# Four projections over one pass of the k tiles, and the scores of two head pairs as one block, in a hybrid HGRN and attention block on one core

## Chip, cores, metric

The kernel runs on one core of one Trainium2 chip. The metric is the device time of one execution in microseconds (us); smaller is better. TensorE, VectorE, ScalarE, GpSimd (POOL) and SyncE (SP) are called PE, DVE, ACT, POOL and SP in the profile.

## The reference

One block of a streaming encoder, fp32, for 256 tokens of width 2048: a mixer of two branches side by side, merged by gates, and after it a squared-ReLU MLP.

```python
def mixer_block(u, w_in, lb, hg_norm_w, rel_bias, w_branch_a, w_branch_b, w_out):
    z = u @ w_in
    hq, hf, hi, hg, aq, ak, av, gates = jnp.split(z, SPLIT_POINTS, axis=-1)
    g = lb + (1.0 - lb) * jax.nn.sigmoid(hf)
    log_g, kk = jnp.log(g), 1.0 - g
    q = jax.nn.silu(hq) * (HG_DK ** -0.5)
    o = hgrn2_scan(q, kk, hi, log_g)                       # 8 heads of 128
    y_a = rms_norm(o, hg_norm_w) * jax.nn.silu(hg)
    y_b = chunk_band_attention(aq, ak, av, rel_bias)       # 16 heads of 64: softmax(q k / 8 + bias) v
    gate_a, gate_b = jnp.split(jax.nn.sigmoid(gates), 2, axis=-1)
    return (gate_a * (y_a @ w_branch_a) + gate_b * (y_b @ w_branch_b)) @ w_out
...
h = x + mixer_block(rms_norm(x, norm_mix_w), ...)
u = rms_norm(h, norm_mlp_w)
h = h + jnp.square(jax.nn.relu(u @ w_up)) @ w_down
return rms_norm(h, norm_final_w)
```

(Heads and shapes are left out above.) The scan's chunks have 64 tokens; with 256 tokens the attention reaches all earlier chunks, and its bias depends on the clipped distance of query and key.

## The kernel before

**Products.** Every fp32 operand is split in two: a high part, rounded by ACT (`split`, L91; now and then by DVE), and a low part, the difference, by DVE (L92). A product is then high by high plus the two mixed terms. The names in the profile follow this: `raw` is a weight tile as loaded by SP (six buffers), `wh` and `wl` its high and low part (four buffers each), `act_x` both parts of the input. `mm3` (L141 to L143) makes a product whose weights are the moving operand, in three matmuls of 512 columns; `mm_t` (L183, L188) makes a transposed one, with the weights stationary. `weights` is the generator that loads and splits; `tc.high_priority` and `tc.issue_after` tell a scheduler where an instruction is to stand in its engine's order. On each engine instructions run strictly in that order.

**Start.** The HGRN projections hf and hq have 1024 columns each, in halves: hf0, hq0, hf1, hq1. The first three are multiplied side by side: a loop over the k tiles loads and splits two k tiles of x (one at a time at the very start) and then gives each projection its matmuls (`for i in range(3)`). Their sums lie in PSUM: hf0 and hq0 in the four banks of `ps_acc`, hf1 in the two of `ps_sm`. After the loop `add_parts` (L194 to L197) makes f0 and q0, the squares of x give 1/rms (`rstd`), and `rows` (to L314) spreads it over the columns with two transposes on PE. Only then hq1 is multiplied, alone, by `gemm_t` over all 16 k tiles; during this time f and q of the first halves are scaled and go through sigmoid, log and exp (`hf_pair`, `hq_pair`). The projections hi and hg follow, and within them the first HGRN scores (L455, L479, L552), whose last operand is `ql` (L545). ACT loads another table of functions when it goes from sigmoid to log, silu or exp (ACT_TABLE_LOAD).

**Attention.** Four units of the gate and attention projections (av, qk, ga0, ga2; each a product made of block products, whose weight blocks and their sums and differences have names such as p21A, p21B, p21D and r_8) each carry the attention of four heads, as two pairs. The steps are hung into the unit's slots, a slot being 12 matmuls of `mm3`, by tables such as `at_slots((2, p0[0]), (4, p0[1]), (7, ...), (9, ...))`: at slot 2 the first pair, at slot 4 the second, at 7 and 9 their transposes, and the values at the start of the next unit. `attn_pair` (L686 to L727) does for a pair: eight small matmuls for the scores (L694; two heads of 64 rows run side by side on the array's halves) into the one buffer of `ps_sc`; POOL loads the bias (two DMAs, L698, and a memset, L699) into `bias`, a tile with one buffer; DVE adds it (L705, one instruction for columns 0 to 127 and one for the rest), takes the maximum (L707), ACT the exp (L710), DVE the reciprocal (L712) and the multiplication (L714); the transposes on PE (L720, `tpp`) come when their slot calls for them. In between DVE makes the low parts of the unit's weights and adds partial sums (L908).

## Time and profile before

| what | value |
|---|---|
| time, median of 3 runs | 1363.72 us (1363.05 to 1364.31) |
| profiled execution | 1363.58 us, of which the span from the first to the last instruction is 1361.9 us |
| busy PE / DVE / ACT / POOL | 1350.3 / 1166.9 / 970.7 / 156.3 us |
| mean granted clock of TensorE | 0.998 |
| DMA | 336.92 MB, mean 247 GB/s |

The profile shows one execution. A row of a timeline has the start, the length, the engine, the line of the kernel, the operation, its output and inputs, and in brackets the idle time ahead of it on its engine, with what ended it. Where rows of one line follow each other, they are drawn as one with their number (x2), and their lengths overlap a little, since an engine starts on an instruction before the one ahead has ended. TensorE's matmuls overlap likewise: their spacing, not their length, is what one costs.

### The profile page before, as it was taken

What the parts mean: (1) busy time and instruction counts of PE and PEld (TensorE: products, weight loads), DVE (VectorE), ACT (ScalarE), POOL (GpSimd) and SP (SyncE); (2) the same over time, 40 slices, a digit from 0 to 9 for tenths busy, and PEclk for the clock granted to TensorE, in tenths of its full rate; (3) what the DMA queues carried; (4) which work ended last, traced back from release to release, by engine and by line L of the source; (5) the groups of instructions that cost most, each with busy time, mean ns of one, the idle gap of its engine ahead of it and who ended that gap; (6) DMA issues with size and microseconds to landing.
All of it is one profiled execution on the core that took longest, in us unless ns stands there. A gap on an engine that the chain in (4) does not pass through costs nothing.

```text
span 1361.9 us, 19182 instructions
## 1 busy us (share of the span) xinstructions
PE 1350.3 (99%) x6753; PEld 1116.1 (82%) x6753; DVE 1166.9 (86%) x1406; ACT 970.7 (71%) x1299; POOL 156.3 (11%) x239
## 2 busy tenths in 40 slices
PE   9999999999999999999999999999999999999997
PEld 7888888878778888888888888888888888888886
DVE  6888977887888988798998889898889988899885
ACT  6877765776777666556778767787667876678764
POOL 3000000110110000110121011100121001110210
PEclk9999999999999999999999999999999999999999
DMA  9655557778885988869898889998899988999892
GB/s 347 228 185 157 176 181 264 217 211 258 247 225 171 307 276 246 262 153 325 286 278 264 244 254 263 281 306 225 245 281 275 301 222 238 294 292 274 260 279 97
DMA packets 132498, 336.92 MB, mean 247 GB/s; under 512 B 11296, under 2 KB 14624, under 8 KB 132016
## 3 DMA queue, kind: packets, MB, share of 16 engines
q1 hardware_dynamic: 110816, 266.11, 56.4%
q0 software_dynamic: 21296, 69.28, 26.2%
q8 instruction: 53, 0.87, 0.2%
q14 instruction: 45, 0.37, 0.1%
q10 hardware_dynamic: 288, 0.29, 0.1%
HBM read 271.67 MB, written 10.49 MB: 207 GB/s over the span
## 4 chain that ended last, share of the span: by engine, by line
PE 98%; DMA 1%; ACT 0%; DVE 0%; issue 0%; SPq 0%; POOL 0%; POOLq 0%; DVEq 0%
PE acc_hq L183 2%; PE acc_hf L183 2%; PE tp_u L110 1%; PE acc_hq L188 1%; PE acc_hg L143 1%; PE acc_hi L143 1%; PE acc_hg L141 1%; PE acc_hi L142 1%; PE acc_hg L142 1%; PE acc_ga2c L141 1%; PE acc_hi L141 1%; PE acc_hf L188 1%; PE acc_ga0c L141 1%; PE acc_avc L141 1%; PE acc_dn30c L141 1%; PE acc_wo2c L143 1%
## 5 line engine op out<-in xcount | busy, mean ns | idle before, releaser
L183 PE MATMUL acc_hq<-act_x,wh_hq 128*128 128x512 f32 x128 | 41.0, 399 | 1.5 <-ACT wh_hq L91 1.2
L183 PE MATMUL acc_hf<-act_x,wh_hf 128*128 128x512 f32 x128 | 40.6, 398 | 0.4 <-DVE wh_hf L91 0.4
L1339 POOL DMA_DIRECT2D hd<-y x24 | 24.7, 1041 | 45.8 <-ACT y L1338 45.4
L188 PEld LDWEIGHTS acc_hf<-act_x,wl_hf 128*128 128x128 f32 x128 | 23.4, 188 | 5.4
L188 PEld LDWEIGHTS acc_hq<-act_x,wl_hq 128*128 128x128 f32 x128 | 23.4, 188 | 5.3 <-DVE wl_hq L92 0.2
L141 PE MATMUL acc_hg<-wh_hg,act_x 128*128 128x512 f32 x64 | 25.1, 392 | 0.0
L141 PE MATMUL acc_hi<-wh_hi,act_x 128*128 128x512 f32 x64 | 25.0, 391 | 0.0
L143 PE MATMUL acc_hg<-wh_hg,act_x 128*128 128x512 f32 x64 | 24.9, 390 | 0.0
L143 PE MATMUL acc_hi<-wh_hi,act_x 128*128 128x512 f32 x64 | 24.9, 389 | 0.0
L142 PE MATMUL acc_hi<-wl_hi,act_x 128*128 128x512 f32 x64 | 24.9, 389 | 0.0
L142 PE MATMUL acc_hg<-wl_hg,act_x 128*128 128x512 f32 x64 | 24.9, 389 | 0.0
L92 DVE TENSOR_TENSOR wl_hq<-raw_hq,wh_hq 128x1024 fp32r<-128x1024 f32 (+2 forms) x21 | 20.1, 966 | 5.4 <-ACT wh_hq L91 5.4
L188 PE MATMUL acc_hq<-act_x,wl_hq 128*128 128x256 f32 x128 | 24.6, 279 | 0.0
L188 PE MATMUL acc_hf<-act_x,wl_hf 128*128 128x256 f32 x128 | 24.6, 279 | 0.0
L92 DVE TENSOR_TENSOR wl_hf<-raw_hf,wh_hf 128x512 fp32r<-128x512 f32 (+2 forms) x26 | 20.9, 811 | 4.1 <-ACT wh_hf L91 3.9
L91 ACT CAST wh_hq<-raw_hq 128x1024 fp32r<-128x1024 f32 (+2 forms) x21 | 17.6, 842 | 8.9 <-DMA raw_hq<-in_w_in_t_dram 4.6
L92 DVE TENSOR_TENSOR act_u<-tp_u,act_u 128x512 fp32r<-128x512 f32 x28 | 19.2, 685 | 5.3 <-ACT act_u L91 5.3
L100 POOL TENSOR_TENSOR ro<-os,mhalf 128x4 f32<-128x4 f32 x4 | 4.4, 1099 | 167.4 <-DVE os L99 164.3
L92 DVE TENSOR_TENSOR wl_hg<-raw_hg,wh_hg 128x1024 fp32r<-128x1024 f32 x16 | 19.4, 1219 | 3.0 <-ACT wh_hg L91 3.0
L183 PEld LDWEIGHTS acc_hq<-act_x,wh_hq 128*128 128x128 f32 x128 | 19.9, 189 | 2.2 <-ACT wh_hq L91 1.4
L183 PEld LDWEIGHTS acc_hf<-act_x,wh_hf 128*128 128x128 f32 x128 | 19.9, 190 | 1.0 <-DVE wh_hf L91 0.7
L91 ACT CAST wh_hf<-raw_hf 128x512 fp32r<-128x512 f32 (+2 forms) x24 | 17.5, 740 | 4.4 <-PE acc_hg L143 1.6
(2295 smaller groups left out, 5327.3 us busy)
## 6 DMA issues: line engine op xcount, KB each, us to landing
raw_hi<-in_w_in_n_dram SPq DMA_DIRECT2D x16, 512.0 KB, 3.8
raw_hg<-in_w_in_n_dram SPq DMA_DIRECT2D x16, 512.0 KB, 3.7
raw_hq<-in_w_in_t_dram SPq DMA_DIRECT2D x12, 512.0 KB, 5.2
hd<-y POOLq DMA_DIRECT2D x24, 256.0 KB, 8.6
raw_hf<-in_w_in_t_dram SPq DMA_DIRECT2D x16, 256.0 KB, 5.6
raw_hf<-in_w_in_t_dram SPq DMA_DIRECT2D x8, 512.0 KB, 4.0
raw_aq<-in_w_in_t_dram SPq DMA_DIRECT2D x8, 512.0 KB, 4.4
raw_ak<-in_w_in_t_dram SPq DMA_DIRECT2D x8, 512.0 KB, 4.3
```

The costliest lines, as they stand in the source:

```text
L91: casts[:] = [(copy or nc.scalar.copy)(hi, src)]
L92: low[:] = [nc.vector.tensor_tensor(lo, src, hi.bitcast(F32), op=ALU.subtract)]
L100: nc.gpsimd.tensor_tensor(dst, ms, mhalf[:, :width], op=ALU.pow)
L110: nc.tensor.transpose(tp[:, j, :], src[:, j * P:(j + 1) * P], ident)
L141: nc.tensor.matmul(acc, hi, wh, start=first, stop=False, skip_group_check=True)
L142: nc.tensor.matmul(acc, hi, wl, start=False, stop=False, skip_group_check=True)
L143: newest[:] = [nc.tensor.matmul(acc, lo, wh, start=False, stop=last, skip_group_check=True)]
L183: newest[:] = [nc.tensor.matmul(acc[cb], wh[:, cb * P:(cb + 1) * P], r.rearrange("p u t -> p (u t)"), start=kt == 0, stop=last)]
L188: newest[:] = [nc.tensor.matmul(acc[cb][:, 0:T], wl[:, cb * P:(cb + 1) * P], r[:, 0, :], start=False, stop=False)]
L1339: nc.gpsimd.dma_start(hd[n][m], t, accum_op=ALU.add)
```

## The change

Two things. First, hq1 joins the loop at the start as a fourth projection; its sums lie in the two banks of `ps_tp`, so the transposes of rstd move to `ps_sm`, and behind the sums of all four projections. hq1's weights are thereby loaded in smaller pieces, as those of the others. Second, `attn_scores` makes the scores of both pairs of a unit at the slot of the first pair: the first pair's into two banks of `ps_tp`, one for each head, the second pair's into `ps_sc`. `attn_pair` begins at the bias; for the first pair the add is made of four instructions (one for each head and span), for the second of two as before. The steps of the units qk and ga2 move by one slot.

```diff
                 nc.scalar.copy(dst[:, cb, :], acc[cb][:, T:])
-                nc.vector.tensor_tensor(dst[:, cb, :], acc[cb][:, 0:T], dst[:, cb, :], op=ALU.add)
+                added = nc.vector.tensor_tensor(dst[:, cb, :], acc[cb][:, 0:T], dst[:, cb, :], op=ALU.add)
+        return added
 
...
     xT = [new_act(f"x{c}") for c in range(4)]
-    accs = [new_acc("hf0"), new_acc("hq0"), [ps_sm.tile([P, NC], F32, name=f"acc_hf1{j}", tag="sm") for j in range(2)]]
+    accs = [new_acc("hf0"), new_acc("hq0")] + [[pool.tile([P, NC], F32, name=f"acc_{what}{j}", tag=tag) for j in range(2)]
+                                               for what, pool, tag in (("hf1", ps_sm, "sm"), ("hq1", ps_tp, "tp"))]
     ws = [weights(w_in_t, C_HF, KD, T, "hf0", (1, 1) + (2,) * 7, first=True),
           weights(w_in_t, C_HQ, KD, T, "hq0", (1, 1) + (2,) * 7),
-          weights(w_in_t, C_HF + T, KD, T, "hf1", (1, 1) + (2,) * 7)]
+          weights(w_in_t, C_HF + T, KD, T, "hf1", (1, 1) + (2,) * 7),
+          weights(w_in_t, C_HQ + T, KD, T, "hq1", (1, 1) + (2,) * 7)]
     steps = [1, 1] + [2] * (KD // 2 - 1)
...
 
-    done = [0, 0, 0]
+    done = [0] * 4
     for kt, n in zip(starts, steps):
...
                                                       op0=ALU.mult, op1=ALU.subtract)
-        for i in range(3):
+        for i in range(4):
             with ExitStack() as es:
...
         nc.vector.tensor_copy(wide, bc(factors, 2, P))
-        tp = ps_tp.tile([P, NM, P], F32, name=f"tp_{what}", tag="tp")
+        tp = ps_sm.tile([P, NM, P], F32, name=f"tp_{what}", tag="sm")
         for m in range(NM):
...
 
-    f0, z0 = h2("f0"), h2("zq0")
-    add_parts(f0, accs[0])
-    add_parts(z0, accs[1])
+    f0, z0, f1, z1 = [h2(what) for what in ("f0", "zq0", "f1", "zq1")]
+    for i, t in enumerate((f0, z0, f1, z1)):
+        added = add_parts(t, accs[i])
     for m in range(NM):
...
     rsqrt(rstd, xsq, D, NM)
-    rstd_t = rows(rstd, "rstd")
+    with tc.issue_after(added.ins):
+        rstd_t = rows(rstd, "rstd")
     rstd8 = const.tile([P, T], F32, name="rstd8")[:, 0:NM]
     nc.vector.tensor_scalar(rstd8, rstd, 0.125, None, op0=ALU.mult)
-
-    f1, z1 = h2("f1"), h2("zq1")
-    add_parts(f1, accs[2])
-    add_parts(z1, gemm_t(xT, w_in_t, C_HQ + T, KD, "hq1"))
 
...
 
-    def attn_pair(g, pr, qT, kT):
+    SPANS = (slice(0, P), slice(P, 3 * P))
+
+    def attn_scores(g, p0, qT, kT):
+
+        first = [ps_tp.tile([P, NC], F32, name=f"s{g}{p0}{j}", tag="tp") for j in range(2)]
+        second = ps_sc.tile([P, 2, NC], F32, name=f"s{g}{p0 + 1}", tag="sc")
+        both = (first, [second[:, j, :] for j in range(2)])
+        with tc.issue_after(newest[0].ins), tc.high_priority(offset=2000):
+            for d, q, k in zip(SPANS, (slice(0, P), slice(P, T)), (slice(0, P), slice(0, T))):
+                for p in range(2):
+                    for j in range(2):
+                        r = slice(64 * j, 64 * j + 64)
+                        nc.tensor.matmul(both[p][j][:, d], qT[r, p0 + p, q], kT[r, p0 + p, k], start=True, stop=True)
+        return ([lambda d, j=j: (slice(j, j + 1), first[j][:, d].rearrange("p (j t) -> p j t", j=1)) for j in range(2)],
+                [lambda d: (slice(0, 2), second[:, :, d])])
+
+    def attn_pair(g, pr, scores):
 
         n = g * 4 + pr
-        sc = ps_sc.tile([P, 2, NC], F32, name=f"s{g}{pr}", tag="sc")
-        with tc.issue_after(newest[0].ins), tc.high_priority(offset=2000):
-            for d, q, k in ((slice(0, P), slice(0, P), slice(0, P)), (slice(P, 3 * P), slice(P, T), slice(0, T))):
-                for j in range(2):
-                    r = slice(64 * j, 64 * j + 64)
-                    nc.tensor.matmul(sc[:, j, d], qT[r, q], kT[r, k], start=True, stop=True)
         bias = bp.tile([P, 2, T], F32, name=f"bias{n}", tag="bias", bufs=1)
...
         s = bp.tile([P, 2, 3 * P], F32, name=f"sb{n}", tag="s", bufs=2)
-        spans = (slice(0, P), slice(P, 3 * P))
+        spans = SPANS
         mx = small.tile([P, 2, 2], F32, name=f"mx{n}", tag="mx")
...
         for d in spans:
-            nc.vector.tensor_tensor(s[:, :, d], sc[:, :, d], rev(bias[:, :, 0:d.stop - d.start]), op=ALU.add)
+            for part in scores:
+                j, sc = part(d)
+                nc.vector.tensor_tensor(s[:, j, d], sc, rev(bias[:, j, 0:d.stop - d.start]), op=ALU.add)
         for b, d in enumerate(spans):
...
         g, p0 = i // 2, i % 2 * 2
-        turns, pts = [], []
+        turns, pts, got = [], [], []
+
+        def scores():
+            got.extend(attn_scores(g, p0, qkT[f"q{g}"], qkT[f"k{g}"]))
 
         def pair(p):
-            qT, kT = [qkT[f"{name}{g}"][:, p0 + p, :] for name in "qk"]
-            turns.extend(attn_pair(g, p0 + p, qT, kT))
-
-        return ([lambda p=p: pair(p) for p in range(2)], [lambda j=j: pts.append(turns[j]()) for j in range(4)],
+            turns.extend(attn_pair(g, p0 + p, got[p]))
+
+        return (scores, [lambda p=p: pair(p) for p in range(2)], [lambda j=j: pts.append(turns[j]()) for j in range(4)],
                 lambda: attn_values(g, p0, (pts[:2], pts[2:]), av[g]))
...
     yb += [new_act(f"yb{g}") for g in range(2)]
-    (p0, t0, v0), (p1, t1, v1), (p2, t2, v2), (p3, t3, v3) = chunks
+    (s0, p0, t0, v0), (s1, p1, t1, v1), (s2, p2, t2, v2), (s3, p3, t3, v3) = chunks
     alone(Unit(lambda: xT, lambda: Sx, w_in_n, C_AV, "av", values,
-               steps=at_slots((0, turn_of("k0")), (2, p0[0]), (4, p0[1]), (7, t0[0], t0[1]), (9, t0[2], t0[3])))) 
+               steps=at_slots((0, turn_of("k0")), (2, s0, p0[0]), (4, p0[1]), (7, t0[0], t0[1]), (9, t0[2], t0[3])))) 
 
...
     alone(Unit(lambda: xT, lambda: Sx, w_in_t, C_AQ + NC, "qk", qk_done, apart=HG,
-               steps=at_slots((0, v0), (1, p1[0]), (3, p1[1]), (6, t1[0], t1[1]), (9, t1[2], t1[3]))))
-    gate_steps = [at_slots((0, turn_of("q1"), v1), (1, turn_of("k1")), (3, p2[0]), (5, p2[1]), (7, t2[0], t2[1]), (9, t2[2], t2[3])),
-                  at_slots((0, v2), (1, p3[0]), (3, p3[1]), (6, t3[0], t3[1]), (8, t3[2], t3[3]), (10, v3))]
+               steps=at_slots((0, v0), (2, s1, p1[0]), (4, p1[1]), (6, t1[0], t1[1]), (9, t1[2], t1[3]))))
+    gate_steps = [at_slots((0, turn_of("q1"), v1), (1, turn_of("k1")), (3, s2, p2[0]), (5, p2[1]), (7, t2[0], t2[1]), (9, t2[2], t2[3])),
+                  at_slots((0, v2), (2, s3, p3[0]), (4, p3[1]), (6, t3[0], t3[1]), (8, t3[2], t3[3]), (10, v3))]
 
```

How the change moves instructions shows in three places. A row has the line, the operation, its output and inputs by the program's names with their buffer numbers, and the size.

**PE, unit av.** Before, around the second pair's scores (`k0T` and `q0T` are the turned keys and queries, `s` the scores in PSUM, `wh_avp21A` and `wh_avr_10` weight blocks of the unit):

```order
L142 MATMUL acc_avc_2788<-wl_avp21A_2930,S_x 128x512
L143 MATMUL acc_avc_2788<-wh_avp21A_2929,S_x 128x512
L694 MATMUL s_2941<-k0T,q0T 128x128 x2
L694 MATMUL s_2941<-k0T,q0T 128x256 x2
L141 MATMUL acc_avc_2817<-wh_avr_10_2965,act_x_105 128x512
L142 MATMUL acc_avc_2817<-wl_avr_10_2966,act_x_105 128x512
```

And now, at the slot of the first pair, which is 24 matmuls earlier:

```order
L143 MATMUL acc_avc_2831<-wh_avp12C_2877,S_x 128x512
L698 MATMUL s_2891<-k0T,q0T 128x128
L698 MATMUL s_2892<-k0T,q0T 128x128
L698 MATMUL s_2893<-k0T,q0T 128x128 x2
L698 MATMUL s_2891<-k0T,q0T 128x256
L698 MATMUL s_2892<-k0T,q0T 128x256
L698 MATMUL s_2893<-k0T,q0T 128x256 x2
L141 MATMUL acc_avc_2831<-wh_avr_8_2923,act_x_105 128x512
```

The second pair's scores (s_2893) have joined the first pair's (s_2891 and s_2892, one bank for each head); at the old place, a slot boundary before wh_avr_10, none are left.

**DVE, unit av.** Before, from the first pair's adds on (`sb` the scores with bias in SBUF, `mx` the maxima, `sum` the sums of exp, `wl_` the low parts of weight blocks, `acc_avc` and `u_av` partial sums of the unit):

```order
L705 TENSOR_TENSOR sb_2886<-s_2877,bias_2882 128x2x128
L705 TENSOR_TENSOR sb_2886<-s_2877,bias_2882 128x2x256
L707 TENSOR_REDUCE mx_2887<-sb_2886 128x2 x2
L92 TENSOR_TENSOR wl_avp21B_2985<-raw_avB_2749,wh_avp21B_2984 128x1024
L92 TENSOR_TENSOR wl_avp21B_2995<-raw_avB_2751,wh_avp21B_2994 128x1024
L705 TENSOR_TENSOR sb_2950<-s_2941,bias_2946 128x2x128
L92 TENSOR_TENSOR wl_avr_8_3007<-rawp_avr_8_2765,wh_avr_8_3006 128x1024
L908 TENSOR_TENSOR acc_avc_2817<-acc_avc_2817,u_av 128x512
L712 RECIPROCAL rs_2897<-sum_2888 128x4
L705 TENSOR_TENSOR sb_2950<-s_2941,bias_2946 128x2x256
L714 TENSOR_TENSOR sb_2886<-sb_2886,rs_2897 128x2x128
```

And now:

```order
L717 TENSOR_TENSOR sb_2906<-s_2891,bias_2902 128x256
L717 TENSOR_TENSOR sb_2906<-s_2892,bias_2902 128x256
L719 TENSOR_REDUCE mx_2907<-sb_2906 128x2 x2
L717 TENSOR_TENSOR sb_2967<-s_2893,bias_2963 128x2x128
L92 TENSOR_TENSOR wl_avp21B_3002<-raw_avB_2763,wh_avp21B_3001 128x1024
L92 TENSOR_TENSOR wl_avp21B_3012<-raw_avB_2765,wh_avp21B_3011 128x1024
L717 TENSOR_TENSOR sb_2967<-s_2893,bias_2963 128x2x256
L920 TENSOR_TENSOR acc_avc_2831<-acc_avc_2831,u_av 128x512
L92 TENSOR_TENSOR wl_avr_8_3024<-rawp_avr_8_2779,wh_avr_8_3023 128x1024
L724 RECIPROCAL rs_2919<-sum_2908 128x4
L92 TENSOR_TENSOR wl_avr_10_3055<-rawp_avr_10_2808,wh_avr_10_3054 128x1024
L726 TENSOR_TENSOR sb_2906<-sb_2906,rs_2919 128x2x128
```

The first half of the second pair's add (128x2x128, reading s_2893 and its bias) has moved from behind both wl_avp21B to ahead of them, and its second half from behind wl_avr_8 to ahead of it. In ga2 the same happens; in ga0 that first half has moved to ahead of wl_ga0r_8 and of a partial sum; in qk both wl_qkp21B stay ahead of it. The first pair's two multiplications (L714, now L726) stood behind wl_avr_8 and behind wl_avr_10; now the second of them follows behind both wl_avp21D. Below the change lines have other numbers: L694 is now L698, L705 is L717, L720 is L732 and L908 is L920.

**ACT, projection hg.** Before, from the cast of its k tiles 6 on (`el`, `er`, `lg`, `sq` are operands of the HGRN scores, the number behind `el` and `er` the level; `v` the evicted hi projection):

```order
L91 CAST wh_hg_6_943<-raw_hg_6_942 128x1024
L425 ACTIVATE v_855<-acc_hi_677,rstd 128x512
L425 ACTIVATE v_857<-acc_hi_678,rstd 128x512
L91 CAST wh_hg_8_972<-raw_hg_8_971 128x1024
L91 CAST wh_hg_10_990<-raw_hg_10_989 128x1024
L498 ACT_TABLE_LOAD
L498 ACTIVATE el_2_1165<-el_2_1165 128x512
```

And now, from just behind the cast wh_hg_8 on:

```order
L425 ACTIVATE v_871<-acc_hi_692,rstd 128x512
L498 ACTIVATE el_8_806<-el_8_806 128x512
L402 ACT_TABLE_LOAD
L402 ACTIVATE lg_969<-f_635 128x512
L91 CAST wh_hg_10_1004<-raw_hg_10_1003 128x1024
L503 ACT_TABLE_LOAD
L503 ACTIVATE er_8_809<-er_8_809 128x16x24
L412 ACT_TABLE_LOAD
L412 ACTIVATE sq_1136<-zq_636 128x512
L91 CAST wh_hg_12_1022<-raw_hg_12_1021 128x1024
L498 ACT_TABLE_LOAD
L498 ACTIVATE el_32_881<-el_32_881 128x512
```

el_8, el_32 and er_8 stood ahead of wh_hg_4 before, and stand behind wh_hg_8 now, with four loads of a table among them; lg and sq of the second half of the heads are among them too.

## Prediction

> **What bounds the kernel now.** I read the profile's page first, then the list of TensorE's waits, then the timelines of the stages that the diff touches. From the page, the busy times and the chain that ended last, by engine:
>
> ```profile
> PE 1350.3 (99%) x6753; PEld 1116.1 (82%) x6753; DVE 1166.9 (86%) x1406; ACT 970.7 (71%) x1299; POOL 156.3 (11%) x239
> ...
> PE 98%; DMA 1%; ACT 0%; DVE 0%; issue 0%; SPq 0%; POOL 0%; POOLq 0%; DVEq 0%
> ```
>
> TensorE's waits (engine, line, releaser: total us, times, longest):
>
> ```profile
> PE acc_hq L183 <- ACT wh_hq L91: 1.2, 1, 1.2
> ...
> PE acc_qkc L141 <- ACT u_qk L872: 0.5, 1, 0.5
> PE acc_hf L183 <- DVE wh_hf L91: 0.4, 1, 0.4
> PE acc_hq L183 <- DVE act_x L297: 0.3, 1, 0.3
> ```
>
> TensorE is the bound everywhere. A change can win only what these few rows hold, or spacing between matmuls. It can lose wherever VectorE, 86% busy and working strictly in its order, becomes late. So each part is asked two things: how much of TensorE's time it removes, and which operand is late next. The sum is made against the profiled execution, 1363.58 us (span 1361.9), 0.14 below the median of 1363.72. A measurement of this kernel can tell about 0.2%, 2.7 us, from no change.
>
> **1. Four projections at the start.** Timeline rows (start, length, engine), and the window of 10 to 20 us (busy PE, PEld, DVE, ACT, POOL, then clock, DMA share, GB/s):
>
> ```profile
> 7.57 0.73 PE L183 MATMUL acc_hq<-act_x,wh_hq 128*128 128x512 f32 x2 [1.17 <-ACT wh_hq L91]
> 9.57 0.47 PE L183 MATMUL acc_hq<-act_x,wh_hq 128*128 128x512 f32 x1 [0.33 <-DVE act_x L297]
> 10.02 0.42 DVE L92 TENSOR_TENSOR wl_hq<-raw_hq,wh_hq 128x256 fp32r<-128x256 f32 x1
> 10.36 0.42 DVE L92 TENSOR_TENSOR wl_hf<-raw_hf,wh_hf 128x256 fp32r<-128x256 f32 x1
> ...
> 10.00:20.00 10.00, 10.00 (x59) 8.66 (x58) 10.00 (x21) 7.68 (x17) 4.12 (x11) 1.00 1.04 374
> ```
>
> The 1.17 wait is for hq0's first piece, which is queued ahead of anything new, so it stays. The 0.33 wait for k tile 1's low x could be filled by hq1's first four matmuls. But they need one more VectorE subtraction, 0.34 us (10.02 to 10.36), and that stands ahead of the low x, so the low x moves out by as much as TensorE gained: I take +0.1, bounds -0.5 (the gap filled) to +0.8 (two more subtractions ahead). Later in the stage a k pair holds four projections where it held three, so VectorE and DMA have more TensorE time to hide in.
>
> The transposes of rstd move from the middle of hq1 to behind the first matmuls of the hi projection; VectorE's copy for them ends about as TensorE gets there. +0.1, bounds 0 to 0.5.
>
> **2. First HGRN scores.** Before, f and q were added and scaled while hq1 was still being multiplied; now all four sums end with the stage. Timeline rows: the scaling rows are ready (46.27), the hi projection starts (52.45), ScalarE's and VectorE's rows, the last operand ql (80.03), the matmul that reads it (92.15).
>
> ```profile
> 46.27 0.42 DVE L314 COPY rows_rstd<-tp_rstd 128x256 f32<-128x256 f32 x1
> 52.45 0.39 PE L141 MATMUL acc_hi<-wh_hi,act_x 128*128 128x512 f32 x1
> 77.92 1.05 ACT L91 CAST wh_hg<-raw_hg 128x1024 fp32r<-128x1024 f32 x1
> 78.22 1.22 DVE L92 TENSOR_TENSOR wl_hg<-raw_hg,wh_hg 128x1024 fp32r<-128x1024 f32 x1
> 80.03 0.35 DVE L545 TENSOR_TENSOR ql<-qr,d 128x192 f32<-128x192 f32 x1
> 82.53 1.28 ACT L498 ACT_TABLE_LOAD   x1 [1.58 <-DVE el L497]
> 83.83 0.64 ACT L498 ACTIVATE el<-el 128x512 f32<-128x512 f32 x1
> 84.36 1.03 ACT L91 CAST wh_hg<-raw_hg 128x1024 fp32r<-128x1024 f32 x1
> 92.15 0.71 PE L552 MATMUL ps<-ql,kc 128*128 128x128 f32 x4
> ```
>
> Before, ql was ready at 80.38, 11.8 us early. Call the start of hi T (52.45). The rows were ready 6 us before T; now the transposes come at about T+5.7, so they are ready some 12.5 us later relative to T, more than the 11.8 in hand. ScalarE's chain then runs without a gap from the cast wh_hg_8, which waits for TensorE to free a buffer (77.92, T+25.0 to 25.5): three casts at 0.94 (1.03 in the row, 0.94 apart back to back), four table loads at 1.29, and six activations and evictions of 0.45 to 0.6, 3.2 in all, make 11.2, T+36.3. VectorE follows with kl, three small q products, two weight subtractions of 1.13 and the last qr, kc and ql, 5.5 us: T+41.9. TensorE asks at T+39.9 (92.15-52.45, and 0.2 for the moved transposes). Stall 2.0; bounds 0 (2 us of the two engines overlap) to 4 (everything falls behind its predecessor).
>
> What ScalarE pays for a table is in the rows: the load starts at 82.53, its activation 1.30 later. The Trainium skill's page ScalarE: Activation LUTs, section What ACT_TABLE_LOAD costs, adds a drain of about 1.38 us to each switch, which speaks against this change: four switches would make the stall an estimated 7.5 in place of 2.0. This trace shows 1.30 from load to activation and no such drain, so the sum goes by 1.30.
>
> **3. One block of scores in place of two.** TensorE around the second pair's scores:
>
> ```profile
> 262.70 0.39 PE L143 MATMUL acc_avc<-wh_avp21A,S_x 128*128 128x512 f32 x1
> 263.01 0.93 PE L694 MATMUL s<-k0T,q0T 64*128 64x128 f32 x8
> 263.87 0.50 PE L141 MATMUL acc_avc<-wh_avr,act_x 128*128 128x512 f32 x1
> 264.21 0.39 PE L142 MATMUL acc_avc<-wl_avr,act_x 128*128 128x512 f32 x1
> ```
>
> From 262.70 to 264.21 are 1.51 us where two matmuls at 0.227 would take 0.45: a block costs 1.06. Its eight passes start over 0.66 us (the pieces of the row, and the next L141 0.86 after the first); the other 0.4 is entry, exit and drain of the last. Two pairs in one block: 1.06+0.66=1.72 for 2.12, so -0.40 per unit and -1.6 over four. Bounds -0.8 (only entry and exit, 0.2, are saved) to -2.1 (all but the passes overlap).
>
> **4. What the one block does to VectorE.** The scores of the second pair are now ready early, and the second pair's add of the bias has moved up in VectorE's order: in unit av it stands ahead of both wl_avp21B, in ga2 too, in ga0 ahead of wl_ga0r_8. But the bias tile has one buffer. POOL can load the second pair's bias only after the first pair's last add, and that pair is not earlier. Unit av (third row: first half of the second pair's add):
>
> ```profile
> 258.81 1.01 DVE L705 TENSOR_TENSOR sb<-s,bias 128x256 f32<-128x256 f32 x2
> 260.41 1.14 POOL L698 DMA_DIRECT2D bias<-in_rel_bias_dram  x2 [8.17 <-DVE mx L707]
> 261.66 2.46 DVE L92 TENSOR_TENSOR wl_avp21B<-raw_avB,wh_avp21B 128x1024 fp32r<-128x1024 f32 x2 [0.91 <-ACT wh_avp21B L91]
> 266.77 0.20 POOL L699 MEMSET bias<- 64x128 f32 x1 [5.23 <-DMA bias<-in_rel_bias_dram]
> 266.96 0.39 PE L142 MATMUL acc_avc<-wl_avp21B,act_x 128*128 128x512 f32 x1
> 267.00 0.42 DVE L705 TENSOR_TENSOR sb<-s,bias 128x256 f32<-128x256 f32 x1 [2.88 <-POOL bias L699]
> 267.34 1.22 DVE L92 TENSOR_TENSOR wl_avr<-rawp_avr,wh_avr 128x1024 fp32r<-128x1024 f32 x1
> 268.48 0.69 DVE L908 TENSOR_TENSOR acc_avc<-acc_avc,u_av 128x512 f32<-128x512 f32 x1
> 271.21 0.68 DVE L714 TENSOR_TENSOR sb<-sb,rs 128x512 f32<-128x512 f32 x1
> 272.18 0.82 PE L720 MATMUL tpp<-ident,sb 128*128 128x128 f32 x6
> ```
>
> Before, VectorE made wl_avp21B at 261.66 and only then idled 2.88 us for the bias, at no cost. Now it idles with wl_avp21B behind it. The bias comes free at R, 267.0 before. From the DMA's end of issue (261.55) to the memset are 5.2 us, the median of these loads:
>
> ```profile
> DMA to landing us min/median/max: 3.3/5.2/6.5
> ```
>
> I take R half a us sooner, 266.5, since SP's loads run dry while VectorE holds their buffers (bounds: as before, or 1.9 sooner by the shortest landing). After R come the half add 0.34, wl_avp21B twice 1.14, the half add 0.6, L908's sum 0.6, wl_avr 1.14 and 1.13, reciprocal 0.1, mult 0.33, two wl_avp21D 1.13 each with another sum 0.6 between, and the last mult 0.6: 10.0, so 276.5. TensorE needs the first wl_avp21B at 266.56 (266.96-0.40) and stalls there already; it asks for the mult (transposes tpp, which stand four matmuls later than before) at 272.18-0.40+0.91=272.7. Stall in all 3.8.
>
> The other units (each with the add that waited, or the matmuls that will):
>
> ```profile
> 364.00 1.02 DVE L705 TENSOR_TENSOR sb<-s,bias 128x256 f32<-128x256 f32 x2 [0.55 <-POOL bias L699]
> 364.46 0.39 PE L142 MATMUL acc_ga0c<-wl_ga0r,act_x 128*128 128x512 f32 x1
> 366.96 0.82 PE L720 MATMUL tpp<-ident,sb 128*128 128x128 f32 x6
> 404.18 0.42 DVE L705 TENSOR_TENSOR sb<-s,bias 128x256 f32<-128x256 f32 x1 [0.53 <-POOL bias L699]
> 410.27 0.82 PE L720 MATMUL tpp<-ident,sb 128*128 128x128 f32 x6
> ```
>
> ga0: R=364.0-0.5=363.5; wl_ga0r_8 is ready after the half add, the sum and itself, 2.1 later, 365.6, for a matmul at 364.06: it stalls. The mult ends 7.7 after R (two subtractions and a sum fewer than 10.0), 371.2; tpp, six matmuls later now, asks at 366.96-0.40+1.36=367.9. Stall 3.3. ga2: its scores come one slot of twelve matmuls (2.72) later, R=404.18+2.72-0.4=406.5; mult at 416.5, tpp (sixteen matmuls later) at 410.27-0.40+3.63=413.5. Stall 3.0. qk: there wl_qkp21B stays ahead of the add and the 0.5 wait in the list goes, while the next subtraction may be late; +0.2, bounds -0.5 to +0.7. The eight extra, shorter adds are 0.15 us more of VectorE per unit, in time in which it waits.
>
> **Sum.** +0.1+0.1+2.0-1.6+3.8+0.2+3.3+3.0=+10.9, so 1363.58+10.9=1374.5. With R up to 0.5 later or 0.7 sooner in three units, the HGRN stall from 1 to 4, and the upper bounds of the start and of qk, 1371 to 1379.5.
>
> **Rivals.**
> A, the bias lands as fast as the fastest load seen: 3.3 for 5.2, so R is 1.4 sooner than taken; the units stall 2.4, 1.9 and 1.6, with nothing at the HGRN scores: 1363.58+0.2-1.6+5.9+0.2=1368.3, with that stall 1370.3; 1367 to 1371. For it: DMA has less to do while VectorE waits. Against: the median is 5.2, with DMA as loaded as here.
> B, ending not slower: the bias is there in time. If its 256 KB share the engines evenly with SP's loads, at half of the 374 GB/s of the window above, they take 1.4 us, R is 3.3 sooner than taken and only av still stalls, 0.5: 1363.58+0.2+2.0-1.6+0.5+0.2=1364.9; without the HGRN stall 1362.9, and with none at all 1362.2. It decides once the landing is under some 2 us. The Trainium skill's page DMA: Bandwidth & Descriptors, section Queues, rings and completion order, has each DMA engine go round between the queues packet by packet, by which POOL's load would get such a share. This trace has no landing of the bias under 3.3.
> C, faster: the start loses its waits (1.2+0.4+0.3) as four projections give more to multiply per k tile, the blocks win their bound of 2.1, nothing stalls: 1363.58-1.9-2.1=1359.6. Against: hq0's wait comes first in the queue.
> D, worse: the bias at its slowest landing (6.5, 1.3 over the median, in three units) and 4 at the HGRN scores: 1374.5+1.5+3.9+2=1382.
>
> **Chances.** Forecast 0.45, A 0.20, B 0.16, C 0.07, D 0.12. The likeliest gives 1374.5. The range 1364 to 1380 leaves out C, the lower half of B and half of D, about 0.2. Faster by over 0.2% (under 1361.0) 0.08: C and a shred of B. Within 0.2% 0.15: the rest of B. Slower 0.77.
>
> **What would show it.** In the profile after, right: "POOL bias" as what ended VectorE's idle time just ahead of the adds in units av, ga0 and ga2, some 4 us each; TensorE waiting at wl_avp21B, wl_ga0r, wl_ga2p21B and at tpp for the mult, 10 us together; a wait of some 2 us at the first HGRN scores; two pairs' scores spanning 1.7 us. Wrong: no VectorE idle for the bias, or idle with TensorE's list still under 4 us; then the time is B's. If TensorE's first 12 us show no wait, C's first half was right.

## The result, and the profile after

| | before | after |
|---|---|---|
| time, median of 4 runs each, on one chip | 1364.01 us (1363.05 to 1364.65) | 1385.38 us (1382.84 to 1386.56) |
| profiled execution / its span | 1363.58 / 1361.9 us | 1385.04 / 1383.3 us |

The ratio is 1.0154, 95% interval 1.0138 to 1.0171: 21.4 us slower. The forecast was 10.9 slower, with a range up to 16.4. The side was right, the size half of what came.

The page after, busy times and the chain that ended last:

```profile
PE 1357.7 (98%) x6753; PEld 1120.9 (81%) x6753; DVE 1168.9 (84%) x1419; ACT 971.7 (70%) x1304; POOL 155.6 (11%) x239
...
PE 86%; DMA 5%; DVE 4%; ACT 2%; issue 2%; SPq 0%; POOL 0%; POOLq 0%; DVEq 0%; ACTq 0%
```

The same 6753 matmuls now keep TensorE busy 7.4 us longer, and the chain runs for 13% over DMA, DVE, ACT and issue, where it was 98% TensorE. So there are two things to find: idle time, and matmuls that take longer. The idle time stands in the list of TensorE's waits (us in total, times, longest):

```profile
PE tpp L732 <- DVE sb L726: 7.1, 4, 2.8
PE acc_avc L142 <- DVE wl_avp21B L92: 2.3, 1, 2.3
PE ps_c L479 <- DVE c L537: 2.1, 1, 2.1
PE acc_ga2c L142 <- DVE wl_ga2p21B L92: 1.4, 1, 1.4
...
PE acc_avc L142 <- DVE wl_avr L92: 0.5, 1, 0.5
PE acc_ga2c L142 <- DVE wl_ga2r L92: 0.4, 1, 0.4
PE ps L552 <- DVE ql L545: 0.4, 1, 0.4
PE acc_ga0c L142 <- DVE wl_ga0r L92: 0.3, 1, 0.3
```

The tpp and wl rows of the units add up to 12.0, those of the HGRN scores (ps_c, ps) to 2.5, two at the start to 1.5 (shown below). The places in the units and at the HGRN scores are those of the prediction, but for wl_avr and wl_ga2r (0.5 and 0.4) and one of the four waits at tpp, told below under unit ga0.

Where the time went is read best from the starts of the stages: the first matmul of each stage in the two timelines, before and after, and how much each stretch became longer. The last three columns are the same difference for three kernels told below: the change's start alone (1), its score block alone (2), the block with two bias buffers (3). (The stretch from hg to unit av takes in the projections aq and ak too.)

| stretch | ends, before | ends, after | predicted | after | (1) | (2) | (3) |
|---|---|---|---|---|---|---|---|
| start, to the hi projection | 52.45 | 55.17 | +0.2 | +2.72 | +5.09 | -0.07 | +0.53 |
| hi, to hg | 74.22 | 77.19 | 0 | +0.25 | +0.29 | 0 | 0 |
| hg with the HGRN scores, to unit av | 244.62 | 252.01 | +2.0 | +4.41 | +2.77 | 0 | +0.02 |
| av | 289.99 | 301.74 | +3.4 | +4.36 | -0.12 | +4.35 | -0.55 |
| qk | 336.84 | 347.32 | -0.2 | -1.27 | -0.83 | -1.27 | -1.27 |
| ga0 | 384.66 | 401.70 | +2.9 | +6.56 | +0.08 | +7.03 | +0.43 |
| ga2 | 432.40 | 453.03 | +2.6 | +3.59 | -0.04 | +2.90 | -0.49 |
| the rest, to the last matmul | 1353.51 | 1375.42 | 0 | +1.27 | +0.47 | +2.23 | +0.23 |
| sum | | | +10.9 | +21.9 | +7.7 | +15.2 | -1.1 |

In qk, 0.83 is the profiled execution of before itself: its wait of 0.5 for u_qk is missing also in (1), which has before's attention. The rest holds single waits of TensorE for the MLP's input that come in one execution and not in another.

**Unit av after**, timelines of VectorE and POOL (whose second pair's bias L708 to L709 loads), then of TensorE:

```profile
267.26 1.00 DVE L719 TENSOR_REDUCE mx<-sb 128x2 f32<-128x256 f32 x2
267.93 1.13 POOL L708 DMA_DIRECT2D bias<-in_rel_bias_dram  x2 [8.30 <-DVE mx L719]
274.49 0.20 POOL L709 MEMSET bias<- 64x128 f32 x1 [5.43 <-DMA bias<-in_rel_bias_dram]
274.72 0.42 DVE L717 TENSOR_TENSOR sb<-s,bias 128x256 f32<-128x256 f32 x1 [6.45 <-POOL bias L709]
275.06 1.22 DVE L92 TENSOR_TENSOR wl_avp21B<-raw_avB,wh_avp21B 128x1024 fp32r<-128x1024 f32 x1
276.33 0.50 PE L142 MATMUL acc_avc<-wl_avp21B,act_x 128*128 128x512 f32 x1 [2.27 <-DVE wl_avp21B L92]
276.67 0.39 PE L143 MATMUL acc_avc<-wh_avp21B,act_x 128*128 128x512 f32 x1
276.90 0.40 PE L141 MATMUL acc_avc<-wh_avp21B,act_x 128*128 128x512 f32 x1
...
284.90 0.85 PE L732 MATMUL tpp<-ident,sb 128*128 128x128 f32 x6 [1.40 <-DVE sb L726]
```

This is the mechanism as forecast: VectorE is free at 268.3 and stands 6.45 us before the second pair's add, since POOL may load the one bias buffer only after the first pair's adds, and the load takes 5.43 to land. Behind the add stands wl_avp21B, for which TensorE waits 2.27, and later the multiplication, for which it waits 1.40.

**The score block after**, in the same unit:

```profile
263.56 0.39 PE L143 MATMUL acc_avc<-wh_avp12C,S_x 128*128 128x512 f32 x1
263.88 1.58 PE L698 MATMUL s<-k0T,q0T 64*128 64x128 f32 x16
...
265.73 0.40 PE L142 MATMUL acc_avc<-wl_avr,act_x 128*128 128x512 f32 x1
```

From 263.56 to 265.73 are 2.17 us, less the 0.45 of two matmuls 1.72, the figure forecast.

**The first HGRN scores after**, TensorE's timeline, and two-us windows of it (busy PE, PEld, DVE, ACT, POOL, then granted clock, DMA share, GB/s):

```profile
96.96 0.57 PE L479 MATMUL ps_c<-qr,kl 128*32 128x96 f32 x24 [2.11 <-DVE c L537]
...
98.92 0.63 PE L142 MATMUL acc_hg<-wl_hg,act_x 128*128 128x512 f32 x1
99.35 0.63 PE L143 MATMUL acc_hg<-wh_hg,act_x 128*128 128x512 f32 x1
...
102.10 0.40 PE L141 MATMUL acc_hg<-wh_hg,act_x 128*128 128x512 f32 x1
102.34 0.39 PE L142 MATMUL acc_hg<-wl_hg,act_x 128*128 128x512 f32 x1
```

```profile
98.00:100.00 2.00, 2.00 (x8) 1.71 (x9) 2.00 (x4) 1.45 (x4) 0.00 (x0) 0.59 0.55 201
100.00:102.00 2.00, 2.00 (x6) 1.56 (x6) 2.00 (x8) 1.49 (x6) 0.00 (x0) 0.55 0.68 209
```

The wait of 2.1 + 0.4 is the forecast's 2.0. What was not in the forecast stands behind it: until 101.9 the matmuls start 0.43 us apart (98.92 to 99.35), later 0.24 (102.10 to 102.34). For about 3.4 us the granted clock is near a half, eight matmuls at 0.2 more each, 1.6 us.

**The start after**, TensorE's timeline:

```profile
5.68 1.22 PE L183 MATMUL acc_hf<-act_x,wh_hf 128*128 128x512 f32 x2 [0.78 <-DVE wh_hf L91]
...
7.13 1.05 PE L183 MATMUL acc_hq<-act_x,wh_hq 128*128 128x512 f32 x2
...
9.37 1.22 PE L183 MATMUL acc_hf<-act_x,wh_hf 128*128 128x512 f32 x2 [0.76 <-ACT wh_hf L91]
...
10.81 1.05 PE L183 MATMUL acc_hq<-act_x,wh_hq 128*128 128x512 f32 x2
...
12.19 1.11 PE L183 MATMUL acc_hf<-act_x,wh_hf 128*128 128x512 f32 x2
...
13.37 0.62 PE L183 MATMUL acc_hq<-act_x,wh_hq 128*128 128x512 f32 x2
...
14.06 0.63 PE L183 MATMUL acc_hf<-act_x,wh_hf 128*128 128x512 f32 x2
```

A group of four matmuls takes 0.69 from 13.37 on (to 14.06), but 1.45 from 5.68, 1.44 from 9.37, 1.38 from 10.81 and 1.18 from 12.19, 2.7 us more for four groups; the one from 7.13 is as slow (two matmuls of 1.05 for 0.62) and adds an estimated 0.5. The listed waits fell from 1.9 to 1.5, and yet hi begins 2.72 later.

**Unit ga0 after**, VectorE's and TensorE's timelines around the second pair's transposes:

```profile
389.94 1.23 DVE L92 TENSOR_TENSOR wl_ga0r<-rawp_ga0r,wh_ga0r 128x1024 fp32r<-128x1024 f32 x1 [2.59 <-ACT wh_ga0r L91]
391.09 1.02 DVE L726 TENSOR_TENSOR sb<-sb,rs 128x256 f32<-128x256 f32 x2
392.25 1.51 PE L732 MATMUL tpp<-ident,sb 128*128 128x128 f32 x6 [2.77 <-DVE sb L726]
393.99 0.63 PE L143 MATMUL acc_ga0c<-wh_ga0r,act_x 128*128 128x512 f32 x1
394.42 0.63 PE L141 MATMUL acc_ga0c<-wh_ga0r,act_x 128*128 128x512 f32 x1
```

The multiplication for these transposes stands behind a low part that waits for ACT, whose cast waits 2.35 for its weight tile to be loaded. In VectorE's order of before it stood ahead of that low part, the unit's last, and of two more. The forecast had followed only the first pair's in this unit; this wait of 2.77 is the second pair's, and slow matmuls follow it too (0.43 apart).

### The profile page after: what moved, and what is told of

It reads as the page before. It is cut to its first block, busy times and chain, and to the rows that moved or that the text cites. A ratio compares the mean times of both kernels' runs of the same rounds, so it can differ in the third digit from the quotient of the medians.

```text
span 1383.3 us, 19212 instructions
## 1 busy us (share of the span) xinstructions
PE 1357.7 (98%) x6753; PEld 1120.9 (81%) x6753; DVE 1168.9 (84%) x1419; ACT 971.7 (70%) x1304; POOL 155.6 (11%) x239
## 4 chain that ended last, share of the span: by engine, by line
PE 86%; DMA 5%; DVE 4%; ACT 2%; issue 2%; SPq 0%; POOL 0%; POOLq 0%; DVEq 0%; ACTq 0%
PE acc_hf L183 1%; PE acc_hq L183 1%; DMA raw_hf<-in_w_in_t_dram 1%; PE acc_qkc L141 1%; PE acc_dn30c L141 1%; PE acc_dn30c L143 1%; PE acc_wo2c L143 1%; PE acc_up00c L141 1%; PE acc_dn20c L143 1%; PE acc_dn00c L143 1%; PE acc_dn32c L143 1%; PE acc_wo2c L141 1%; PE acc_dn32c L141 1%; PE acc_up00c L143 1%; PE acc_dn10c L141 1%
## 5 line engine op out<-in xcount | busy, mean ns | idle before, releaser
L722 ACT ACTIVATE sb<-sb,mx 128x128 f32<-128x128 f32 (+1 forms) x32 | 14.3, 448 | 12.7 <-DVE mx L719 12.7
L717 DVE TENSOR_TENSOR sb<-s,bias 128x256 f32<-128x256 f32 (+2 forms) x24 | 9.0, 417 | 15.3 <-POOL bias L709 15.3
L92 DVE TENSOR_TENSOR wl_hq<-raw_hq,wh_hq 128x512 fp32r<-128x512 f32 (+2 forms) x26 | 20.8, 813 | 0.9 <-ACT wh_hq L91 0.8
```

The source lines that it names most:

```text
L92: low[:] = [nc.vector.tensor_tensor(lo, src, hi.bitcast(F32), op=ALU.subtract)]
L717: nc.vector.tensor_tensor(s[:, j, d], sc, rev(bias[:, j, 0:d.stop - d.start]), op=ALU.add)
L722: nc.scalar.activation(s[:, j, d], s[:, j, d], AF.Exp, bias=mx[:, b, j:j + 1], accum_out=sums[:, b, j:j + 1])
```

## The experiments

Two theories stood after the result. The first: the two parts of the change are separate and add up, the start costing about a third and the units two thirds; the units' part is the one bias buffer, and what the forecast lacked is a cost at the start and one behind each wait. The rival: the parts need each other, or something else in the units (the sixteen score matmuls, the shorter adds, the moved slots) costs what the bias buffer was blamed for. Each ratio below is against runs of the kernel before on the same chip, with its 95% interval.

**1. The start alone**: the change's four projections, with before's attention.

> Only the four projections side by side (with the transposes of rstd moved), the attention as before. Theory (two separate losses: a cold start and late HGRN scores here, the bias wait in the attention units): the trace of the changed kernel is 7.4 us late when the aq projection begins, so this kernel takes 1364.0+7.4=1371.4 us, 1369 to 1373.5, with a wait of some 2 us at the first HGRN scores and matmuls at about 0.43 us spacing in the first 12 us and for some 3 us behind that wait. Rival (the four projections cost only my predicted 2.2, and the rest of the lateness comes with the attention's part): 1366.2.

Measured: 1370.75 us (1370.52 to 1371.12), ratio 1.0050 [1.0036, 1.0064]. As expected: this third is a cost of its own. Its trace shows one cause that the trace of after hides. ScalarE's timeline, then TensorE's, near the end of the loop:

```profile
44.91 1.91 ACT L280 ACTIVATE xr<-xr 128x2048 f32<-128x2048 f32 x1 [4.53 <-DMA xr<-in_x_dram]
46.82 0.60 ACT L91 CAST wh_hf<-raw_hf 128x512 fp32r<-128x512 f32 x1
47.47 1.11 PE L183 MATMUL acc_hf<-act_x,wh_hf 128*128 128x512 f32 x2 [2.47 <-ACT wh_hf L91]
...
48.80 1.06 PE L183 MATMUL acc_hf<-act_x,wh_hf 128*128 128x512 f32 x2
```

The squares of x (L280; 128x2048 of fp32 to load, 1 MB) stand in ScalarE's order ahead of the last casts of the loop. ScalarE idles 4.53 us for the load with those casts behind it, TensorE waits 2.47 for the cast and then runs at half speed (two matmuls take 1.06 from 48.80, for 0.62 in the rows of the start). In before, whose ScalarE timeline this row is from, the squares stand behind the loop's last cast (31.24) and ahead of hq1's first (36.19), and wait for nothing, as the missing bracket says:

```profile
32.28 1.92 ACT L277 ACTIVATE xr<-xr 128x2048 f32<-128x2048 f32 x1
```

In after ScalarE waits 2.19 for the same load, but TensorE is itself late by its slow first matmuls and asks that much later: no wait of TensorE's for the last casts is in its list. The two losses of the start stand for one another.

**2. The score block alone**: before's start, the change's attention.

> Only the score block of two pairs, the start as before. Theory: the changed kernel loses 13.3 us between the start of aq and the start of gb0, so 1364.0+13.3=1377.3 us, 1375.5 to 1379.5, all of it TensorE waits at wl of the blocks 21B and r and at the transposes tpp, and a slow stretch behind the longest of them. Rival (the parts are not additive: the late start is what makes the attention's loads collide): under 1374.

Measured: 1374.72 us (1373.83 to 1378.05), ratio 1.0083 [1.0070, 1.0097], a little under the band. Its waits at tpp are 6.2, at wl_avp21B 2.3. TensorE behind that one:

```profile
268.88 0.69 PE L142 MATMUL acc_avc<-wl_avp21B,act_x 128*128 128x512 f32 x1 [2.27 <-DVE wl_avp21B L92]
269.37 0.63 PE L143 MATMUL acc_avc<-wh_avp21B,act_x 128*128 128x512 f32 x1
269.80 0.63 PE L141 MATMUL acc_avc<-wh_avp21B,act_x 128*128 128x512 f32 x1
```

The same wait of the same length, 2.27, is followed by matmuls 0.43 apart here and 0.23 apart in after (276.67 to 276.90). The slow stretch is not certain to follow a wait.

**10 and 11. Both repeated on another chip**: the block alone, and the whole change.

> The score block alone once more, since its four times lay 4 us apart. Theory (the times scatter with the clock behind the long waits and with single waits of 1 to 2 us in the MLP, which the profiles of several kernels have or have not): median 1374 to 1376.5, single times from 1373 to 1378.

> The changed kernel once more beside the block alone. Theory (the two parts lose independently, 7.1 and 11): 1382 to 1385. Rival (part of the loss comes only where both are together): 1385 or more, with the block alone under 1375.

Measured: 1377.74 us (1375.49 to 1379.13), ratio 1.0101 [1.0086, 1.0116], 1.2 above its band, and 1382.62 (1381.73 to 1386.16), ratio 1.0147 [1.0129, 1.0166]. Start alone +7.1, block alone +11.1 and +14.4, together +19.3 and +21.4: the parts add up within their scatter, which is wide (on the chip of runs 10 and 11 the whole change has only 4.9 more than the block).

**3. The block with two bias buffers.** Room for it comes from two tiles that were larger, or lived longer, than their data need.

```diff
-        bias = bp.tile([P, 2, T], F32, name=f"bias{n}", tag="bias", bufs=1)
+        bias = bp.tile([P, 2, T], F32, name=f"bias{n}", tag="bias", bufs=2)
...
-        r = const.tile([P, T], F32, name=f"rows_{what}")
+        r = hp.tile([P, T], F32, name=f"rows_{what}")
...
-    rstd8 = const.tile([P, T], F32, name="rstd8")[:, 0:NM]
+    rstd8 = const.tile([P, NM], F32, name="rstd8")
```

> The score block with a bias tile of two buffers (the room comes from a tile of 256 columns of which 2 were used, and from a pool that ends earlier), the start as before. Theory (the wait for the one bias buffer is the whole loss of the attention part): no TensorE waits in the four units, and the blocks' gain of 0.4 each is left: 1362.4 us, 1361.8 to 1363.2. Rival (the scores of the first pair hold the two banks that the transposes need, or the eight more adds make VectorE late): the waits at tpp stay, 1370 or more.

Measured: 1362.91 us (1361.37 to 1364.29), ratio 0.9994 [0.9985, 1.0003]. One number takes away what the block cost, 11.8 us of the median. VectorE in unit av:

```profile
259.37 1.14 DVE L717 TENSOR_TENSOR sb<-s,bias 128x128 f32<-128x128 f32 x4
...
261.35 1.01 DVE L717 TENSOR_TENSOR sb<-s,bias 128x256 f32<-128x256 f32 x2
```

The second pair's adds follow without idle time. The rival falls with that: the sixteen matmuls, the shorter adds and the moved slots are all still there. Of the units' waits one is left, 0.4 for u_ga in ga0, which before does not have. So the blocks win 0.55, 0.44 (1.27 less the 0.83 of before's own wait) and 0.49 in av, qk and ga2; in ga0 the new wait takes the gain back.

**4. Before with two bias buffers**: the same three edits, nothing else.

> The kernel before, with the bias tile of two buffers alone. Theory: VectorE's idle time for the bias goes, but nothing on TensorE waited for it except the one 0.5 us: 1363.5 us, within 0.6 of before. Rival (the second buffer is a gain of its own, so that the kernel with block and two buffers owes it its time): 1362.4 or less.

Measured: 1364.51 us (1362.11 to 1366.90), ratio 1.0004 [0.9995, 1.0013], 0.3 above its band and not different from before. The second buffer is worth nothing by itself: what kernel 3 repairs is the block's own wait.

**9. The block with one bias buffer, but the second pair's add kept behind the unit's low parts**, by slot and by order (the slots of av are shown; those of the other three units move alike):

```diff
+        with ExitStack() as es:
+            if pr % 2:
+                es.enter_context(tc.issue_after(lows[-1].ins))
...
-               steps=at_slots((0, turn_of("k0")), (2, s0, p0[0]), (4, p0[1]), (7, t0[0], t0[1]), (9, t0[2], t0[3])))) 
+               steps=at_slots((0, turn_of("k0")), (2, s0, p0[0]), (6, p0[1]), (7, t0[0], t0[1]), (9, t0[2], t0[3])))) 
...
```

> The score block alone, still with one bias buffer, but the second pair's bias and adds taken up two slots later, so that in VectorE's order they stand behind both weight parts wl of the block 21B (av, ga2) and wl of r (ga0), as they did before. Theory (the buffer's load takes what it takes, but what is queued behind the add on VectorE decides the price): the waits at 21B go, those at the transposes shrink since fewer operations stand between the add and the multiplication; of some 11 us lost, 3 to 6 stay: 1367 to 1370. Rival (what costs is the one buffer itself, wherever the add stands, since the second pair's softmax is late for its transposes): 1373 or more.

Measured: 1371.45 us (1369.42 to 1376.48), ratio 1.0062 [1.0040, 1.0085]: between the two. The waits at wl_avp21B and wl_avr are gone, as the order says, but the transposes pay: 7.5 in five waits, since the pair's add, and so its multiplication, now comes later. With one buffer the order chooses who waits, and saves a part (8.1 above before, where the block alone has 14.4 on the same chip); it does not take the wait away.

**5 and 6. What the start is made of.** Kernel 1 with the squares behind the loop's last casts, and kernel 1 with the first HGRN scores 12 matmuls later:

```diff
-        squares(m)
+        with tc.issue_after(casts[0].ins):
+            squares(m)
```

```diff
-    s0 = scores(0, a0[0], 5, 15, ((5, a1[1]), (8, a1[2])))
+    s0 = scores(0, a0[0], 5, 19, ((5, a1[1]), (8, a1[2])))
```

> The four projections alone, with ScalarE's squares of x placed behind the last casts of the stage and no longer ahead of four of them. Theory (TensorE's 2.5 us wait before the last k tiles is the square that waits for its 1 MB load with the casts behind it, and the slow matmuls behind the wait are its consequence): the wait goes and 3.7 us with it, from 1370.75 to 1367.0, 1366 to 1368.5; the wait of 2.1+0.4 at the HGRN scores stays. Rival (the stage is short of weight loads, with raw buffers for one and a half k groups only, and the square merely shows it): 1369.5 or more.

> The four projections alone, with the first HGRN scores placed four ticks (twelve matmuls, 2.7 us) later in TensorE's order. Theory (their operands are 2.5 us late because everything behind the sums starts later; nothing else depends on it): the wait goes, 1370.75-2.5=1368.2, 1366.8 to 1368.8, the lower end if the wait had slowed the matmuls behind it in most runs. Rival (the chain of VectorE and ScalarE only follows, since what it makes next is late by as much): 1370 or more, with the wait at the second scores.

Measured: 1369.27 us (1366.11 to 1370.07), ratio 1.0035 [1.0022, 1.0047], and 1368.45 (1366.69 to 1370.66), ratio 1.0034 [1.0022, 1.0046]. Kernel 5's waits:

```profile
PE ps_c L480 <- DVE c L538: 2.1, 1, 2.1
...
PE tp_rstd L315 <- DVE wide_rstd L312: 1.1, 1, 1.1
```

With the squares later, hi begins only 0.36 later than in before (5.09 in kernel 1), but rstd is later too: 1.1 at its transposes, and the wait at the scores is followed by half speed (granted clock 0.52 and 0.63 from 96 to 100 us). Between the two expectations: a cost removed there was in part given back downstream. Kernel 6 came as expected: the waits at the first HGRN scores are gone and the squares' wait (3.7 in its trace) is still there. In the four profiles with the squares ahead of the last casts (after and kernels 1, 6 and 11) hi begins 2.72 to 6.75 late, in the two with them behind (5 and 7) 0.36 and 0.84.

**7. The whole change with the three repairs** (two bias buffers, squares later, scores later).

> The whole change, with three mends: two bias buffers, the squares behind the casts, the first HGRN scores twelve matmuls later. Theory (these three are the whole loss): 1370.75-3.7-2.5-0.7=1363.8, 1362.5 to 1365.5, so no loss against before and hardly a gain. Rival (something of the start is left, such as early waits for pieces that now land in a longer queue): 1366 or more.

Measured: 1365.29 us (1363.81 to 1369.50), ratio 1.0012 [1.0003, 1.0021], within its band. Of 21.4 us 1.3 are left, most of it at the start: hi begins 0.84 late, for waits of 0.9, 0.7 and 0.3 at the first pieces and some slow matmuls behind them.

**8. A colder start by itself**: before with one warming matmul (L81) in place of eight.

> The kernel before with one of its eight warming matmuls in place of eight. Theory (TensorE's matmuls run at half speed until some microseconds of work have gone by, whatever the profile's clock shows there): the first 3 to 4 us of real matmuls take about 0.43 us each in place of 0.23, and 1 to 3 us are lost: 1365 to 1367. Rival (the slow matmuls at the start of the changed kernel came from late operands): no change, within 0.5 of before.

TensorE's timeline at its start, and under it that of kernel 3, whose start is that of before with all eight:

```profile
5.67 1.22 PE L183 MATMUL acc_hf<-act_x,wh_hf 128*128 128x512 f32 x2 [3.75 <-DVE wh_hf L91]
...
5.28 1.22 PE L183 MATMUL acc_hf<-act_x,wh_hf 128*128 128x512 f32 x2 [0.37 <-DVE wh_hf L91]
```

Measured: 1365.82 us (1364.29 to 1367.35), ratio 1.0013 [1.0004, 1.0022], 1.9 above before, as expected. The first matmuls are as slow here as in after (1.22 for two), but only 0.53 of the loss lies in the start of the profiled execution; where the rest comes from is not shown. And the same slow rows stand in kernel 3, and in 10 and 12, which also have before's start: hi begins 0.5 to 0.6 late in these three, and not late in kernels 2, 4 and 9. So a slow start comes in some executions without the change and without fewer warming matmuls. That the four projections bring it on, or make it longer, is not shown.

**12. Kernel 3 again, on another chip.**

> The score block with two bias buffers once more, since 0.7 us under before lay within the interval. Theory (the blocks save 0.44 each, as its trace shows, and a 0.5 us wait goes while one of 0.4 comes): 1362.4 to 1363.2 beside before at 1363.6, a ratio of 0.9991 to 0.9997. Rival (no gain that can be measured): 0.9998 or more.

Measured: 1362.38 us (1361.14 to 1364.34), ratio 0.9992 [0.9983, 1.0001]. Both intervals of this version include 1, so it is not shown to be faster than before. Both medians lie 0.7 to 0.9 under, and the stretches agree: the four units are 1.9 shorter than in the profiled execution of before, 1.0 without its chance wait in qk.

## Why the forecast had the side right and the size wrong

**The units' stall** (forecast 3.8, 0.2, 3.3, 3.0): right in mechanism, 12.0 us of listed waits for 10.3 (4.2, 0, 4.6, 3.2). Kernel 3 shows the cause, and kernel 4 that it is not the buffer for itself. That the sum came so near is in part luck: two steps were off, and in ga0 they offset each other. "I take R half a us sooner" failed in av: VectorE's add begins at 274.72, which less the 7.39 by which the unit began late is 267.3, 0.3 after before's 267.0. In ga0 R came 1.0 sooner than taken, in ga2 0.75 later, and VectorE's idle time for the bias was 6.45, 1.74 and 5.55 in av, ga0 and ga2 for the "some 4 us each" of the prediction. The landing of the bias after, in the view of that tile for the four units:

```profile
DMA to landing us min/median/max: 3.3/5.5/7.1
```

The median is 0.3 more than before's, the slowest 0.6 more. (The view counts from the start of an issue, the prediction's 5.2 from the issue's end; by the view's count the load of unit av took 5.8 before.) So rival B fell, and A in av and ga2; in ga0 the load landed in the 3.3 of A, and the first pair's waits there, 0.3 and 1.5, are near A's 1.9. The even share between queues, which the prediction took from the Trainium skill's page DMA: Bandwidth & Descriptors, section Queues, rings and completion order, would have landed it in an estimated 1.4; no landing shows that. And in ga0 only the first pair was followed: it waited 1.8 for the 3.3 forecast, and the second pair's 2.77 is missing from the sum.

**The score blocks** (-0.40 each): right, 1.72 us a block, and 0.44 to 0.55 won where nothing waits instead.

**The HGRN scores** (stall 2.0): right. VectorE's timeline after has the copy of the scaling rows:

```profile
61.27 0.42 DVE L317 COPY rows_rstd<-tp_rstd 128x256 f32<-128x256 f32 x1 [0.65 <-PE tp_rstd L315]
```

It starts 6.1 behind the start of hi (61.27 less 55.17), where before it started 6.2 ahead: 12.3 later, for the forecast's 12.5. TensorE had c at 41.8 behind the start of hi (96.96 less 55.17) and waited 0.4 more for ql; the forecast had the last operands at 41.9. A table load is 1.28 in ScalarE's timeline after, with its activation 1.29 behind its start:

```profile
82.71 1.28 ACT L402 ACT_TABLE_LOAD   x1
84.00 0.63 ACT L402 ACTIVATE lg<-f 128x512 f32<-128x512 f32 x1
```

By the drain of the Trainium skill's page ScalarE: Activation LUTs, section What ACT_TABLE_LOAD costs, the stall would have been an estimated 7.5; it was 2.5.

**The start** (+0.1 and +0.1): the first failed; the second held, with no wait at the transposes of rstd after (before, they stood at the start of hq1, 41.05, not in its middle as the prediction has it). In the part on the four projections the sentence was "Later in the stage a k pair holds four projections where it held three, so VectorE and DMA have more TensorE time to hide in." It counted two engines and left out ScalarE, on which the squares of x stand, and SP, which loads them; with hq1 in the loop they had moved from behind the loop's last casts to ahead of them. hi began 2.72 late in after, 5.09 in kernel 1, 3.82 in kernel 11, 0.36 with the squares moved (kernel 5). The bounds of that part went to +1.3. In the profile of after itself the 2.72 are slow matmuls (3.2 us) and not waits: the term counted operands alone and had no price for TensorE's speed.

**What a wait does afterwards**: no step of the prediction had it. Two costs, both read from spacing. First, each wait is longer than its row says. The idle time is counted from the end of the matmul ahead, 0.39 long, where the next would have begun 0.23 behind its start; and the first matmul after it takes 0.34 (276.33 to 276.67) for 0.23. That is 0.16 + 0.11 = 0.27 a wait. In the units of after nine waits and in HGRN two make 3.0. Second, half speed, in after 1.6 at the HGRN scores; about 1.4 in ga0 (the six transposes are 1.51 long for the 0.85 of unit av, and four matmuls lose 0.2 each); and some 2.9 at the start (3.2 less the two waits' share). Slow first matmuls come in kernels 3, 10 and 12 too, which have before's start; hi begins 0.5 to 0.6 late there.

**The sum as the runs showed it**, after against before's profiled execution: waits of the units and HGRN 14.5, less before's 0.5 in qk, so 14.0; waits at the start -0.4; 0.27 for each wait, nine more than in before, 2.4; slow matmuls 5.9; four blocks at -0.44, -1.8; the stretch hi to hg 0.25 and the rest 1.3. Together 21.7, of the 21.9 in the table. The forecast's terms cover 10.9; the waits were priced about right in sum, and the half speed and the tails of waits, together 8.3, were priced at nothing. That is also why the range was too low: its upper end summed longer waits, never what follows one. Rival D's 1382 comes nearest in number, but not by its mechanism: the loads landed at 5.5 in the median, and the HGRN scores waited 2.5 and not 4.

Left open: why the half-speed stretch follows some waits and not others, and what makes the first matmuls slow in some executions. The 0.27 is worked out from rows and fits the stretches; no run tried it alone.

## What to carry to other kernels

When an operation is made ready early, look which of its other operands can't be: a scheduler that orders by readiness of one moves it ahead of urgent work, where it blocks the engine until the slower operand lands; here a second buffer was the whole repair of the units. Price each new TensorE wait of some 2 us at up to twice its length, for the restart and the matmuls at half speed behind it. And when a loop takes in work that used to stand behind it, list what had been hidden under that work, on every engine and queue.

## What the runs showed of the hardware

Behind waits of 2.0 to 3.7 us TensorE ran for about 3.4 us with 512-column matmuls 0.43 us apart in place of 0.23, at a granted clock of 0.50 to 0.63, but not each time: behind 2.27 in unit av yes in kernel 2, no in after; behind 2.1 at the HGRN scores yes in after and kernel 5, no in kernels 1 and 11; behind the second pair's wait in ga0 yes in after (2.77), no in kernel 11 (2.58). It fits this that the four runs of kernel 9 go with the mean granted clock: 1369.42 at 0.999, 1370.64 at 0.998, 1372.26 at 0.997, 1376.48 at 0.994. The Trainium skill's page TensorE: Matmul & The Clock Gate, section Part 1: The HAM clock gate, describes a clock halved after an idle window of some 3.4 us and restored after as long a busy one, with windows that run freely. The trace agrees on the halving (0.43 for 0.23) and on the 3.4 us of slow matmuls; but waits well under 3.4 us were enough, and at the start of after, where the spacing is 0.43, the window of 6 to 8 us shows a granted clock of 1.00 (the figure ahead of the last two):

```profile
6.00:8.00 2.00, 2.00 (x7) 1.61 (x7) 0.51 (x2) 0.41 (x1) 1.89 (x8) 1.00 0.88 306
```

So a slow start is seen in the spacing of the rows, not in that column.
